# A hybrid decoder layer on one core: the state-space layer's token-independent matrices made beside the first gate/up products and stored, its recurrence stepped at half products

## The chip, the cores and the metric

The kernel runs on one core of a Trainium2 chip. The metric is the time of one execution on the device, in microseconds (us), as the median of several runs. The engines are TensorE (PE; its weight loads are listed apart as PEld), VectorE (DVE), ScalarE (ACT), GpSimd (POOL) and SyncE (SP), which in this kernel issues the data DMAs. Each engine takes its instructions strictly in the order of the program.

## The reference, cut to what matters

One layer over x (1024 tokens x 1024 channels, float32): FFN, mixer of two gated branches, FFN, final norm. The change touches the state-space (S5) branch of the mixer, and the place of the attention branch's work beside it.

```
x = x + 0.5 * swiglu(rms_norm(x, ffn1_norm), ffn1_w_gate, ffn1_w_up, ffn1_w_down)
h = rms_norm(x, mix_norm);  z = h @ w_in
q, k, v, u, g_attn, g_ssm = ...            # slices of z; the gates after a sigmoid
...
# S5: 32 groups of 16 channels, each drives a 64-dim complex diagonal state
bb = coef * b                              # from lam, dt, b: no token enters
s[t] = ab * s[t-1] + bb u[t]               # complex, per group
y_s = gelu(Re(c s) + d u)
glu = y_s @ ssm_w_glu;  y_s = glu[:, :512] * sigmoid(glu[:, 512:])
y_ssm = y_s @ w_ssm_branch
...
# attention: 3 dilated groups of 4 heads; the 3 outputs of a head are mixed by a
# softmax over the groups' log-denominators (lse)
w_grp = softmax(lse over groups);  o_attn = sum(w_grp * o);  y_attn = o_attn @ w_attn_branch
x = x + (g_attn * y_attn + g_ssm * y_ssm) @ w_out
x = x + 0.5 * swiglu(rms_norm(x, ffn2_norm), ...)
```

## The kernel before

**Products.** Every large product is made of three passes over operands that are split into a high and a low part (`mm3`, L179 to L181; `split`, L83 to L90: ACT makes the high part at L86, DVE the low part at L87). Large matrices go by a seven-product scheme on half blocks (`sevens`, L430, sums at L446, L448 and, of weights, at L353). One product of it (`product`, L400) is 12 matmuls on 128x512 tiles; after 6 of them the generator yields `MID`, after 12 it yields again. I call these two places half products.

**Stages.** PE runs through them in this order: the first FFN's gate/up products (`gate_up`, to about 475 us), its down products (`down`, to about 700 us), the mixer's input projection (`project`, to about 1206 us), the state-space branch's output products (`ssm_out`, to about 1334 us), the attention branch's (`attn_out`), the output matrix (`out_product`), and the second FFN.

**Side work.** `run(main, *side, often=())` (L1667) steps through a main generator, and at each of its yields takes one step of each side generator: at `MID` only of those in `often`. So what a side generator issues between two of its yields stands in each engine's queue between two products (or half products) of the main work. Nothing else sets the order.

```
for x in main:
    for s in list(side):
        if (x != MID or s in often) and next(s, "end") == "end":
```

**S5.** Beside the first gate/up products, from step 50 on, `s5_base` (L791) makes the tables that need no token: powers of the diagonal (PW), the input and output matrices (BB, CT). Beside `project`, `s5_all` (L1153) goes through four tiles of eight groups each (`s5_tile`, L1007), one step per product:

1. U, the tile's inputs, are loaded back from DRAM in a regrouped form (L1021, 8 DMAs).
2. Twelve DVE operations on 128x512 (L1034 to L1039) make W (inputs to chunk states) and CA (states to outputs), three to a step. PE transposes W (L1046), ACT copies it into WT.
3. PE makes the taps within a chunk (L1056, L1060); they go through `ks` to DRAM (Kd, L1067) and come back regrouped as KT (L1084, 8 DMAs).
4. PE multiplies U with WT to the chunk's inputs Vs (L1075).
5. The recurrence within a chunk: seven times four DVE operations on 128x128 (L1096 to L1099), two of these sets of four to a step. Then a doubling scan over the chunks' ends (L1108 to L1111) and its spread into the states (L1124, L1125).
6. PE makes the outputs Y from U, KT, Vs and CA (L1136, L1138); they are stored to Yd (L422, 8 DMAs), and the next tile begins.

SP issues all these DMAs in the program's order, the weight loads of the main work (L345 in the projection) among them.

**Attention.** `att_all` (L1373) starts when all four S5 tiles are done. It is in `often`, at a pace that `fast` sets. The two `combine` (L1309), one for each half of the head pairs, mix the groups: loads of lse sums (L1327), a chain of small DVE operations (L1330 to L1342), stores to Ad (L1349), then for each of three groups a load of the output (`uo`, L1357) and two of the weights (`al`, L1359), a POOL multiplication (L1364) and, from the second group on, a POOL addition (L1367); a last split into ohi and olo (L89, L90) feeds `attn_out`. The second `combine` runs beside the last products of `ssm_out`. Between its DMAs the gate loads `gs` (L1492) and the weight loads of the output matrix (L1545) stand on SP.

Of the kernel before, what the change touches and what calls it, by code (L numbers as in the profile page):

```python
# [55 lines left out]
def tile_layer(ctx: ExitStack, tc: tile.TileContext, w, out: bass.AP, taps=None):  # L56
# [676 lines left out]
    def later(n, gen):  # L733
        for _ in range(n):
            yield
        yield from gen
# [264 lines left out]


    Ud, Yd = dt_((4, 128, 1024), "Ud"), dt_((4, 128, 1024), "Yd")

    late5 = Stores()

    def s5_tile(ut):  # L1007
        q4 = slice(4 * ut, 4 * ut + 4)

        def v4(t):  # L1010
            return t.rearrange("p (q j c) -> p q j c", q=4, j=T5)

        def bj(x):
            return x[:, q4, None, :].to_broadcast([128, 4, T5, 16])

        while len(saved) < 5 or ("u", ut) not in saved:
            yield
        yield
        U = slot("U").rearrange("p (g x) -> p g x", g=8)
# [6 lines left out]
        CAv = [CA[:, 512 * i:512 * i + 512] for i in range(2)]  # L1026
        t1 = half_slot("t1")

        def pw(i, lo):
            return PW[:, i, q4, lo:lo + T5, None].to_broadcast([128, 4, T5, 16])  # L1030

        for o, X_, lo, sg in ((W, BB, 0, 1), (CAv, CT, 1, -1)):

            V.tensor_tensor(out=v4(o[0]), in0=bj(X_[:, 0]), in1=pw(0, lo), op=OP.mult)  # L1034
            V.tensor_tensor(out=v4(t1), in0=bj(X_[:, 1]), in1=pw(1, lo), op=OP.mult)
            V.tensor_tensor(out=o[0], in0=o[0], in1=t1, op=OP.subtract if sg > 0 else OP.add)
            V.tensor_tensor(out=v4(o[1]), in0=bj(X_[:, 1]), in1=pw(0, lo), op=OP.mult)
            V.tensor_tensor(out=v4(t1), in0=bj(X_[:, 0]), in1=pw(1, lo), op=OP.mult)
            V.tensor_tensor(out=o[1], in0=o[1], in1=t1, op=OP.add if sg > 0 else OP.subtract)  # L1039
            yield  # L1040

        WT = slot("WT")
        for i in range(2):
            pt = bank(6 + i)
            for q in range(4):
                P.transpose(pt[:, 128 * q:128 * q + 128], W[i][:, 128 * q:128 * q + 128], ident)  # L1046
            A.copy(out=WT[:, 512 * i:512 * i + 512], in_=pt)
        del W, t1, o, X_
        yield

        pk = bank(6)
        for q in range(4):
            o = pk[32 * q:32 * q + 32]
            for i in range(2):
                lh = BD[:, i, 4 * ut + q].rearrange("p a c -> p (a c)")
                P.matmul(o[:, 0:16], lhsT=lh, rhs=CT[:, i, 4 * ut + q, :], start=i == 0, stop=i == 1,  # L1056
                         tile_position=(0, 32 * q))
            for i in range(2):
                lh = BD[:, i, 4 * ut + q].rearrange("p a c -> p (a c)")
                P.matmul(o[:, 16:128], lhsT=lh, rhs=CAv[i][:, 128 * q:128 * q + 112], start=i == 0,  # L1060
                         stop=i == 1, tile_position=(0, 32 * q))
        ks = half_slot("ks")[:, :256]
        G.memset(ks[:, :128], 0.0)
        V.scalar_tensor_tensor(ks[:, 128:144], DEL, DC[:, ut:ut + 1], pk[:, 0:16], op0=OP.mult, op1=OP.add)
        V.tensor_copy(out=ks[:, 144:256], in_=pk[:, 16:128])
        yield
        nc.sync.dma_start(out=Kd[ut], in_=ks)  # L1067
        del ks

        Vs = slot("Vs").rearrange("p (i q m) -> p i q m", i=2, q=4)  # L1070
        for i in range(2):
            pt = bank(6 + i)
            for q in range(4):
                for g2 in range(2):
                    P.matmul(pt[64 * g2:64 * g2 + 64, 128 * q:128 * q + 128],  # L1075
                             lhsT=WT[:, 512 * i + 128 * q + 64 * g2:512 * i + 128 * q + 64 * g2 + 64],
                             rhs=U[:, 2 * q + g2, :], start=True, stop=True)
            A.copy(out=Vs[:, i], in_=pt)
        del WT
        yield  # L1080
        yield
        KT = slot("KT").rearrange("p (g x) -> p g x", g=8)
        for jr in range(T5):
            nc.sync.dma_start(out=KT[16 * jr:16 * jr + 16],  # L1084
                              in_=bass.AP(tensor=Kd.tensor, offset=Kd.offset + ut * 32768 + 16 + 16 * jr,
                                          ap=[[256, 16], [4096, 8], [1, 128]]))

        Vr = Vs.rearrange("p i q (k m) -> p i q k m", m=T5)
        m12 = half_slot("m12")
# [3 lines left out]
        for m in range(1, T5):  # L1093
            cur = Vr[:, :, :, :, m]
            prev = Vr[:, :, :, :, m - 1]
            V.tensor_tensor(out=m1, in0=prev, in1=ar[:, None, :, None].to_broadcast([128, 2, 4, 16]), op=OP.mult)  # L1096
            V.tensor_tensor(out=m2, in0=prev[:, ::-1], in1=AIS[:, :, q4, None].to_broadcast([128, 2, 4, 16]), op=OP.mult)
            V.tensor_tensor(out=m1, in0=m1, in1=m2, op=OP.add)
            V.tensor_tensor(out=cur, in0=cur, in1=m1, op=OP.add)  # L1099
            if m % 2 == 0:  # L1100
                yield

        E = m12[:, 256:384].rearrange("p (i q k) -> p i q k", i=2, q=4)
        V.tensor_copy(out=E[:, :, :, 0:15], in_=Vr[:, :, :, 0:15, T5 - 1])
        for j in range(4):
            n = 15 - (1 << j)
            pr, n1, n2 = E[:, :, :, 0:n], m1[:, :, :, 0:n], m2[:, :, :, 0:n]
            V.tensor_tensor(out=n1, in0=pr, in1=ARE[:, None, q4, j:j + 1].to_broadcast([128, 2, 4, n]), op=OP.mult)  # L1108
            V.tensor_tensor(out=n2, in0=pr[:, ::-1], in1=AIE[:, :, q4, j:j + 1].to_broadcast([128, 2, 4, n]), op=OP.mult)
            V.tensor_tensor(out=n1, in0=n1, in1=n2, op=OP.add)  # L1110
            V.tensor_tensor(out=E[:, :, :, 15 - n:15], in0=E[:, :, :, 15 - n:15], in1=n1, op=OP.add)  # L1111
            if j % 2:
                yield
        t2 = half_slot("t2")[:, :480].rearrange("p (q k m) -> p q k m", q=4, k=15)

        def bE(i):
            return E[:, i, :, 0:15, None].to_broadcast([128, 4, 15, T5])

        def bA(i):
            return AW[:, i, q4, None, :].to_broadcast([128, 4, 15, T5])  # L1120

        for o, a, b, op in ((0, 0, 0, OP.add), (0, 1, 1, OP.subtract), (1, 0, 1, OP.add), (1, 1, 0, OP.add)):
            for q in range(4):
                V.tensor_tensor(out=t2[:, q], in0=bA(a)[:, q], in1=bE(b)[:, q], op=OP.mult)  # L1124
            V.tensor_tensor(out=Vr[:, o, :, 1:16, :], in0=Vr[:, o, :, 1:16, :], in1=t2, op=op)  # L1125
            yield
        del t2, m12, m1, m2, E, n1, n2, pr
# [181 lines left out]
    def combine(hp):  # L1309

        def vw(t, d):
            return t if d == 1 else t.rearrange("p (r i) -> p i r", r=d)

        def nat(t, d):
            return t if d == 1 else t.rearrange("p (i r) -> p i r", r=d)
# [16 lines left out]
        for g, d in enumerate(DIL):  # L1332
            V.tensor_tensor(out=nat(Eg[:, g], d), in0=vw(R[g][:, 0], d), in1=nat(M, d), op=OP.subtract)
        A.activation(out=Eg, in_=Eg, func=AF.Exp)
        for g, d in enumerate(DIL):
# [3 lines left out]
        V.tensor_tensor(out=nat(M, 16), in0=nat(M, 16), in1=vw(R[2][:, 1], 16), op=OP.add)  # L1339
        V.reciprocal(out=M, in_=M)  # L1340
        for g, d in enumerate(DIL):
            V.tensor_tensor(out=vw(AL[:, g], d), in0=nat(Eg[:, g], d), in1=nat(M, d), op=OP.mult)  # L1342
# [431 lines left out]
    def late_half():  # L1774
# [20 lines left out]
    def ssm_first(k):  # L1795
        while len(freed) < k + 1:
# [73 lines left out]
```

## Time and profile before

| what | value |
|---|---|
| median of 3 runs | 2127.29 us (2123.85 to 2128.09) |
| the profiled execution's own time | 2128.07 us |
| span of the profiled execution | 2126.3 us |
| PE busy | 2020.7 us, 95% of the span |
| DVE busy | 1532.4 us, 72% |
| ACT busy | 804.8 us, 38% |
| POOL busy | 432.8 us, 20% |
| DMA moved | 272.07 MB, mean 128 GB/s |

How to read it: PE is the engine that nearly always works, so time is gained only where PE stands still or runs at a lower granted clock, and lost where the change makes it do so. The other engines' totals count only through the places at which PE waits for them. Matmuls overlap, so a busy PE can hide a small loss; the spacing of matmuls shows it, about 0.226 us for one of 128x512 (332 matmuls in a stretch of 75 us without an idle moment).

### The profile page before, as it was taken

Reading aid. Unit: us, or ns where it says so; the run is one execution under the profiler, and the core shown is the slowest. Engines: PE = TensorE matmul, PEld = TensorE weight load, DVE = VectorE, ACT = ScalarE, POOL = GpSimd, SP = SyncE. Lnnn points to the kernel's source line nnn. Section 1 sums busy time; section 2 is a strip of 40 time slices with the busy share of each in tenths; the row PEclk is TensorE's granted clock in tenths of the full one; section 3 lists DMA queues with packets and bytes.
Section 4 is the critical chain, followed back from the end, with each engine's and each line's share of the span. In section 5 each row is a group of like instructions: output and inputs, shape, how many; then the busy total and the mean of one; then the engine's idle time right before and its main releaser. Section 6 shows DMA issues by size and latency. Waiting matters only on the chain. (4 is left out here: it accounts for less than half of the span.)

```text
span 2126.3 us, 26610 instructions
## 1 busy us (share of the span) xinstructions
PE 2020.7 (95%) x9359; PEld 1619.7 (76%) x9359; DVE 1532.4 (72%) x2764; ACT 804.8 (38%) x1534; POOL 432.8 (20%) x380
## 2 busy tenths in 40 slices
PE   6799999999999899999999999998999999999988
PEld 5687888887877687777777667776788888887866
DVE  7778889768867878777855544626876776769776
ACT  5432322325336422222244653435423223235353
POOL 2022112125531000000000324520121121217350
PEclk9899999999999899999999999998999999999999
DMA  4144333329325133333343655431233333266432
GB/s 158 45 129 138 111 99 111 112 96 350 126 76 175 70 119 112 93 111 105 107 146 123 205 165 170 189 109 60 99 99 100 99 124 99 89 217 238 144 116 83
DMA packets 179562, 272.07 MB, mean 128 GB/s; under 512 B 23576, under 2 KB 110436, under 8 KB 179428
## 3 DMA queue, kind: packets, MB, share of 16 engines
q1 hardware_dynamic: 169008, 264.54, 36.7%
q10 hardware_dynamic: 10308, 5.81, 1.1%
q8 instruction: 74, 1.21, 0.2%
q14 instruction: 60, 0.49, 0.1%
q0 software_dynamic: 112, 0.02, 0.1%
HBM read 191.50 MB, written 81.17 MB: 128 GB/s over the span
## 5 line engine op out<-in xcount | busy, mean ns | idle before, releaser
L179 PE MATMUL bank<-T,wp 128*128 128x512 f32 x1008 | 399.8, 397 | 12.5 <-DVE F L309 8.5
L181 PE MATMUL bank<-T,wp 128*128 128x512 f32 x1008 | 396.1, 393 | 9.7 <-DVE wp L87 9.7
L180 PE MATMUL bank<-T,wp 128*128 128x512 f32 x1008 | 395.2, 392 | 0.0
L87 DVE TENSOR_TENSOR wp<-wraw,wp 128x512 fp32r<-128x512 f32 x400 | 329.7, 827 | 71.2 <-ACT wp L86 69.9
L86 ACT CAST wp<-wraw 128x512 fp32r<-128x512 f32 x400 | 244.4, 620 | 279.9 <-DVE wraw L353 161.7
L179 PE MATMUL bank<-b,wp 128*128 128x512 f32 x756 | 303.7, 402 | 17.3 <-DVE s L446 15.5
L181 PE MATMUL bank<-b,wp 128*128 128x512 f32 x756 | 298.4, 395 | 4.7 <-DVE wp L87 4.7
L181 PE MATMUL bank<-wp,ap 128*128 128x512 f32 x744 | 294.0, 395 | 6.8 <-DVE ap L87 6.1
L180 PE MATMUL bank<-b,wp 128*128 128x512 f32 x756 | 297.6, 394 | 0.0
L180 PE MATMUL bank<-wp,ap 128*128 128x512 f32 x744 | 292.4, 393 | 5.3 <-DVE wp L87 5.3
L179 PE MATMUL bank<-wp,ap 128*128 128x512 f32 x744 | 293.0, 394 | 3.6 <-ACT ap L86 2.5
L179 PEld LDWEIGHTS bank<-T,wp 128*128 128x128 f32 x1008 | 190.6, 189 | 57.4 <-issue 15.1
L181 PEld LDWEIGHTS bank<-T,wp 128*128 128x128 f32 x1008 | 190.8, 189 | 53.4 <-DVE wp L87 12.9
L180 PEld LDWEIGHTS bank<-T,wp 128*128 128x128 f32 x1008 | 190.7, 189 | 38.5
L86 ACT CAST wp<-S 128x512 fp32r<-128x512 f32 x189 | 116.7, 618 | 234.7 <-DVE S L353 185.9
L87 DVE TENSOR_TENSOR wp<-S,wp 128x512 fp32r<-128x512 f32 x189 | 150.5, 797 | 71.2 <-ACT wp L86 70.6
L561 POOL TENSOR_TENSOR S<-sg 128x512 f32<-128x512 f32 x22 | 33.7, 1533 | 779.6 <-DVE sg L547 495.5
L179 PEld LDWEIGHTS bank<-b,wp 128*128 128x128 f32 x756 | 144.0, 191 | 54.5 <-ACT wp L86 12.2
L181 PEld LDWEIGHTS bank<-wp,ap 128*128 128x128 f32 x744 | 140.7, 189 | 43.7 <-DVE ap L87 14.9
L181 PEld LDWEIGHTS bank<-b,wp 128*128 128x128 f32 x756 | 143.7, 190 | 38.4 <-DVE wp L87 7.4
L180 PEld LDWEIGHTS bank<-wp,ap 128*128 128x128 f32 x744 | 140.9, 189 | 37.0 <-DVE wp L87 8.1
L179 PEld LDWEIGHTS bank<-wp,ap 128*128 128x128 f32 x744 | 140.8, 189 | 34.3 <-ACT ap L86 3.9
(251 smaller groups left out, 2826.4 us busy)
## 6 DMA issues: line engine op xcount, KB each, us to landing
araw<-aD SPq DMA_DIRECT2D x154, 256.0 KB
wraw<-in_ffn_w_gate_dram SPq DMA_DIRECT2D x44, 512.0 KB
wraw<-in_ffn_w_up_dram SPq DMA_DIRECT2D x44, 512.0 KB
aD<-sg SPq DMA_DIRECT2D x88, 256.0 KB
wraw<-in_ffn_w_down_dram SPq DMA_DIRECT2D x44, 512.0 KB
wraw<-in_w_in_dram SPq DMA_DIRECT2D x38, 512.0 KB
aD<-S SPq DMA_DIRECT2D x66, 256.0 KB
x<-in_x_dram SPq DMA_DIRECT2D x16, 512.0 KB
```

The costliest lines, as they stand in the source:

```text
L86: A.copy(out=hi, in_=src)
L87: (e or V).tensor_tensor(out=lo, in0=src, in1=hi.bitcast(F32), op=OP.subtract)
L179: P.matmul(pt, lhsT=lhs[0], rhs=rhs[0], start=start, stop=False, skip_group_check=more)
L180: P.matmul(pt, lhsT=lhs[0], rhs=rhs[1], start=False, stop=False, skip_group_check=more)
L181: P.matmul(pt, lhsT=lhs[1], rhs=rhs[0], start=False, stop=stop, skip_group_check=more)
L561: G.tensor_tensor(out=ab[o], in0=ab[a], in1=ab[b], op=op)
```

## The change

The twelve DVE operations per tile, the transposes and the taps are taken out of `s5_tile` into a new generator `s5_weights`, which runs right behind `s5_base` as one side generator (`s5_all_weights`) of the first gate/up products, with one DVE operation to a step. WT and CA go to two new DRAM tiles (WTd, CAd) and are loaded by `s5_tile`: WT behind U, CA behind the recurrence together with KT. What is left of this generator when the gate/up products end is stepped beside the first `down`. `s5_all` is now in `often`, so its steps come at half products; the recurrence yields after the two multiplications and again after the two additions. `combine` gets two more yields.

```diff
+    WTd, CAd = dt_((4, 128, 1024), "WTd"), dt_((4, 128, 1024), "CAd")
...
+    def s5_weights():
+        for ut in range(4):
...
+            CAv = []
+            for X_, lo, sg in ((BB, 0, 1), (CT, 1, -1)):
+                for i in range(2):
+                    o, t1 = half_slot("W"), half_slot("t1")
+                    V.tensor_tensor(out=v4(o), in0=bj(X_[:, i]), in1=pw(0, lo), op=OP.mult)
+                    yield
+                    V.tensor_tensor(out=v4(t1), in0=bj(X_[:, 1 - i]), in1=pw(1, lo), op=OP.mult)
+                    yield
+                    V.tensor_tensor(out=o, in0=o, in1=t1, op=OP.subtract if (sg > 0) == (i == 0) else OP.add)
+                    yield
+                    if sg > 0:
+                        pt = bank(6)
+                        for q in range(4):
+                            P.transpose(pt[:, 128 * q:128 * q + 128], o[:, 128 * q:128 * q + 128], ident)
+                        wt = half_slot("WT")
+                        A.copy(out=wt, in_=pt)
+                        late5.add(WTd[ut][:, HALF[i]], wt)
+                    else:
+                        CAv.append(o)
+                        late5.add(CAd[ut][:, HALF[i]], o)
...
+            late5.add(Kd[ut], ks)
+            yield
+    def s5_all_weights():
+        yield from s5_base()
+        for _ in s5_weights():
+            late5.step()
+            yield
...
     def s5_tile(ut):
...
-        W, CA = two("W"), slot("CA")
...
-            yield
-        yield
-        nc.sync.dma_start(out=Kd[ut], in_=ks)
-        del ks
+        nc.sync.dma_start(out=WT, in_=WTd[ut])
+        for _ in range(5):
+            yield
...
             A.copy(out=Vs[:, i], in_=pt)
+            yield
...
             V.tensor_tensor(out=m2, in0=prev[:, ::-1], in1=AIS[:, :, q4, None].to_broadcast([128, 2, 4, 16]), op=OP.mult)
+            yield
             V.tensor_tensor(out=m1, in0=m1, in1=m2, op=OP.add)
             V.tensor_tensor(out=cur, in0=cur, in1=m1, op=OP.add)
-            if m % 2 == 0:
-                yield
+            yield
+        KT, CA = slot("KT").rearrange("p (g x) -> p g x", g=8), slot("CA")
...
+        nc.sync.dma_start(out=CA, in_=CAd[ut])
...
         A.activation(out=Eg, in_=Eg, func=AF.Exp)
+        yield
...
         V.tensor_tensor(out=nat(M, 16), in0=nat(M, 16), in1=vw(R[2][:, 1], 16), op=OP.add)
+        yield
         V.reciprocal(out=M, in_=M)
...
-    drain(run(gate_up(H, late_half()), later(30, other_gains()), later(40, bias_tables()), later(50, s5_base())))
+    side = run(gate_up(H, late_half()), later(30, other_gains()), later(40, bias_tables()), later(50, s5_all_weights()))
...
-    drain(run(down(NF // 2, tile_of(xin), 0.5, *normed(X1), half0),
+    drain(run(down(NF // 2, tile_of(xin), 0.5, *normed(X1), half0), *side,
...
-    side = run(project(H, later(0, h_seven(1, 1, (1, 2, 6, 7), H)), freed), s5_all(),
+    side = run(project(H, later(0, h_seven(1, 1, (1, 2, 6, 7), H)), freed), s5,
...
-               often=(att,))
+               often=(att, s5))
```

Three places show how this moves instructions. The first is DVE's queue at the start of the first `down`, where the last tile's operations stand between the low halves of the main work (L87, `wp` of one factor and `ap` of the other). Before, nothing else stood there:

```order
L87 TENSOR_TENSOR wp<-wraw,wp 128x512
L87 TENSOR_TENSOR ap<-araw,ap 128x512
L87 TENSOR_TENSOR wp<-wraw,wp 128x512
L87 TENSOR_TENSOR ap<-araw,ap 128x512
L87 TENSOR_TENSOR wp<-wraw,wp 128x512
L87 TENSOR_TENSOR ap<-araw,ap 128x512
```

With the change, rows 741 to 751 of that queue are:

```order
L87 TENSOR_TENSOR wp<-wraw,wp 128x512
L87 TENSOR_TENSOR ap<-araw,ap 128x512
L1032 TENSOR_TENSOR W<-W,t_4219 128x512
L87 TENSOR_TENSOR wp<-wraw,wp 128x512
L87 TENSOR_TENSOR ap<-araw,ap 128x512
L1028 TENSOR_TENSOR W<-CT,PW 128x512
L1030 TENSOR_TENSOR t_4294<-CT,PW 128x512
L1032 TENSOR_TENSOR W<-W,t_4294 128x512
L1028 TENSOR_TENSOR W<-CT,PW 128x512
L87 TENSOR_TENSOR wp<-wraw,wp 128x512
L87 TENSOR_TENSOR ap<-araw,ap 128x512
```

Of the 48 moved operations 17 stand behind the end of the gate/up products; PE's queue has that end at position 1848, and the last matmul of the main work ahead of the last of the 17 operations' users at position 2017.

The second place is SP's queue in the projection, between the stores of one tile's Y and the first loads of the next. Before:

```order
L422 DMA Pdq<-pr 128x1024 x2
L422 DMA Yd<-Y 16x8x128 x8
L1021 DMA U<-Ud 16x8x128 x8
L345 DMA wraw<-in_w_in_dram 128x4x256 x2
L422 DMA Pdk<-pr 128x1024
L1067 DMA Kd<-ks 128x256
L422 DMA Pdk<-pr 128x1024
L1084 DMA KT<-Kd 16x8x128 x8
```

With the change:

```order
L422 DMA Pdq<-pr 128x1024 x2
L422 DMA Yd<-Y 16x8x128 x8
L1080 DMA U<-Ud 16x8x128 x8
L1083 DMA WT<-WTd 128x1024
L345 DMA wraw<-in_w_in_dram 128x4x256 x2
L422 DMA Pdk<-pr 128x1024 x2
L345 DMA wraw<-in_w_in_dram 128x4x256 x2
L422 DMA Pdv<-pr 128x1024 x2
```

WT (512 KB) is loaded right behind U; in the next tile one weight load stands between the stores of Y and U as well. On PE, the first matmuls of Vs (L1075, now L1092) stood 72 matmuls of the main work behind the previous tile's last Y matmul, and now stand 42 behind it (tiles 1 to 3).

The third place is the second `combine` on SP. Before, four gate loads (`gs`) stand behind the first load of `uo`:

```order
L1349 DMA Ad<-c_10671 8x16x8 x2
L1492 DMA gs<-Gd 128x1024
L1357 DMA uo<-Od 128x1024
L1359 DMA al<-Ad 64x1024 x2
L1545 DMA wraw<-in_w_out_dram 128x1024
L1492 DMA gs<-Gd 128x1024 x2
L1357 DMA uo<-Od 128x1024
L1359 DMA al<-Ad 64x1024 x2
L1545 DMA wraw<-in_w_out_dram 128x1024
L1492 DMA gs<-Gd 128x1024 x2
L1357 DMA uo<-Od 128x1024
L1359 DMA al<-Ad 64x1024 x2
```

With the change one does, and three loads of the first `combine` (`uo`, `al` x2) now stand ahead of the second one's lse loads:

```order
L1371 DMA Ad<-c_10798 8x16x8 x2
L1567 DMA wraw<-in_w_out_dram 128x1024
L1514 DMA gs<-Gd 128x1024
L1379 DMA uo<-Od 128x1024
L1381 DMA al<-Ad 64x1024 x2
L1514 DMA gs<-Gd 128x1024
L1567 DMA wraw<-in_w_out_dram 128x1024
L1379 DMA uo<-Od 128x1024
L1381 DMA al<-Ad 64x1024 x2
L1379 DMA uo<-Od 128x1024
L1381 DMA al<-Ad 64x1024 x2
```

The attention's last matmul (L1240, now L1260) moves as well: it stood in front of the last 210 main matmuls of `ssm_out`, and now stands in front of the last 168. The number of main matmuls is the same, 8004.

## Rows read from the trace of the kernel before

**Rows 1.** Profile page, part 1: busy time, share, instructions of each engine.

```profile
PE 2020.7 (95%) x9359; PEld 1619.7 (76%) x9359; DVE 1532.4 (72%) x2764; ACT 804.8 (38%) x1534; POOL 432.8 (20%) x380
```

**Rows 2.** Stretches: length, busy time (count) of each engine, PE clock, DMA share, GB/s.

```profile
200.00:400.00 200.00, 198.21 (x877) 162.97 (x876) 171.34 (x387) 56.79 (x101) 32.42 (x22) 1.00 0.35 108
400.00:475.00 75.00, 75.00 (x332) 62.10 (x332) 50.96 (x69) 24.61 (x44) 12.09 (x8) 1.00 0.34 113
475.00:500.00 25.00, 25.00 (x111) 20.42 (x110) 17.09 (x21) 9.25 (x15) 6.47 (x5) 1.00 0.90 343
500.00:510.00 10.00, 10.00 (x45) 8.26 (x45) 7.98 (x7) 7.78 (x15) 7.96 (x6) 1.00 1.03 414
510.00:560.00 50.00, 48.48 (x210) 38.72 (x209) 50.00 (x42) 22.12 (x38) 37.18 (x23) 1.00 0.44 156
786.00:1090.00 304.00, 286.48 (x1483) 225.90 (x1483) 233.78 (x513) 80.02 (x136) 0.62 (x3) 0.99 0.36 114
```

**Rows 3.** PE's waits, 786 to 1090 us: total us, times, longest us.

```profile
PE bank L181 <- DVE wp L87: 8.0, 8, 2.2
PE bank L179 <- DVE s L446: 4.8, 4, 2.6
PE bank L179 <- DVE pr L1432: 3.9, 2, 2.4
```

**Rows 4.** Timeline of DVE inside the recurrence: start us, us, operation.

```profile
809.13 0.39 DVE L1096 TENSOR_TENSOR m<-Vs,AW 128x128 f32<-128x128 f32 x1
...
810.64 0.40 DVE L1096 TENSOR_TENSOR m<-Vs,AW 128x128 f32<-128x128 f32 x1
...
812.03 0.68 DVE L87 TENSOR_TENSOR wp<-S,wp 128x512 fp32r<-128x512 f32 x1
...
813.37 0.39 DVE L1096 TENSOR_TENSOR m<-Vs,AW 128x128 f32<-128x128 f32 x1
...
817.46 0.39 DVE L1096 TENSOR_TENSOR m<-Vs,AW 128x128 f32<-128x128 f32 x1
```

**Rows 5.** Stretches at 733, 737 and 976 us, columns as in rows 2.

```profile
733.50:737.50 4.00, 0.57 (x3) 0.15 (x1) 4.00 (x7) 1.53 (x3) 0.00 (x0) 1.00 0.00 0
737.50:744.30 6.80, 5.38 (x13) 4.21 (x14) 6.73 (x12) 3.23 (x7) 0.00 (x0) 0.50 0.00 0
976.40:979.80 3.40, 3.40 (x10) 2.63 (x9) 3.30 (x8) 0.00 (x0) 0.00 (x0) 0.50 0.31 107
```

**Rows 6.** Groups of PE's weight loads, 780 to 1090 us: busy, mean ns, idle before.

```profile
L1056 PEld LDWEIGHTS bank<-CT,BD 128*32 128x32 f32 x64 | 2.7, 110 | 1.4 <-issue 1.4
```

**Rows 7.** Timeline of DVE at the start of `down`.

```profile
500.27 0.68 DVE L87 TENSOR_TENSOR ap<-araw,ap 128x512 fp32r<-128x512 f32 x1
500.93 1.72 DVE L87 TENSOR_TENSOR wp<-wraw,wp 128x512 fp32r<-128x512 f32 x1
502.58 1.77 DVE L87 TENSOR_TENSOR ap<-araw,ap 128x512 fp32r<-128x512 f32 x1
```

**Rows 8.** Timeline of PE where tile 0's Y ends.

```profile
856.22 0.50 PE L179 MATMUL bank<-T,wp 128*128 128x512 f32 x1
```

**Rows 9.** Timeline of SP's queue there: start us, us of issuing.

```profile
860.70 3.70 SPq L1021 DMA_DIRECT2D U<-Ud  x8
864.73 0.40 SPq L345 DMA_DIRECT2D wraw<-in_w_in_dram  x1
```

**Rows 10.** The stretch behind that load, columns as in rows 2.

```profile
868.20:870.80 2.60, 2.60 (x13) 2.01 (x12) 2.57 (x5) 1.34 (x3) 0.00 (x0) 1.00 0.00 0
```

**Rows 11.** Timelines at the end of `ssm_out`: PE, SP, POOL and ACT.

```profile
1335.75 0.49 PE L179 MATMUL bank<-ohi,whi 128*128 128x512 f32 x1 [0.72 <-ACT ohi L89]
...
1306.11 1.09 SPq L1359 DMA_DIRECT2D al<-Ad  x2
...
1313.57 2.40 POOL L1364 TENSOR_TENSOR o<-uo,al 128x1024 f32<-128x1024 f32 x1 [10.71 <-DMA al<-Ad]
...
1321.33 2.40 POOL L1364 TENSOR_TENSOR al<-uo,al 128x1024 f32<-128x1024 f32 x1 [3.00 <-DMA al<-Ad]
1323.81 2.97 POOL L1367 TENSOR_TENSOR o<-o,al 128x1024 f32<-128x1024 f32 x1
...
1334.64 1.06 ACT L89 ACTIVATE ohi<-o 128x1024 fp32r<-128x1024 f32 x1 [8.77 <-POOL o L1367]
```

More of the change, by code (lines that the diff above doesn't have):

```diff
@@ L1003, in tile_layer, with v4, bj, pw @@
     Ud, Yd = dt_((4, 128, 1024), "Ud"), dt_((4, 128, 1024), "Yd")
+    WTd, CAd = dt_((4, 128, 1024), "WTd"), dt_((4, 128, 1024), "CAd")
     late5 = Stores()
+    def v4(t):
+        return t.rearrange("p (q j c) -> p q j c", q=4, j=T5)
+    def s5_weights():
+        for ut in range(4):
+            q4 = slice(4 * ut, 4 * ut + 4)
+            def bj(x):
+                return x[:, q4, None, :].to_broadcast([128, 4, T5, 16])
+            def pw(i, lo):
+                return PW[:, i, q4, lo:lo + T5, None].to_broadcast([128, 4, T5, 16])
+            CAv = []
[18 more added lines that the diff above has]
+                        late5.add(CAd[ut][:, HALF[i]], o)
+            pk = bank(6)
+            for q in range(4):
+                o = pk[32 * q:32 * q + 32]
+                for i in range(2):
+                    lh = BD[:, i, 4 * ut + q].rearrange("p a c -> p (a c)")
+                    P.matmul(o[:, 0:16], lhsT=lh, rhs=CT[:, i, 4 * ut + q, :], start=i == 0, stop=i == 1,
+                             tile_position=(0, 32 * q))
+                for i in range(2):
+                    lh = BD[:, i, 4 * ut + q].rearrange("p a c -> p (a c)")
+                    P.matmul(o[:, 16:128], lhsT=lh, rhs=CAv[i][:, 128 * q:128 * q + 112], start=i == 0,
+                             stop=i == 1, tile_position=(0, 32 * q))
+            ks = half_slot("ks")[:, :256]
+            G.memset(ks[:, :128], 0.0)
+            V.scalar_tensor_tensor(ks[:, 128:144], DEL, DC[:, ut:ut + 1], pk[:, 0:16], op0=OP.mult, op1=OP.add)
+            V.tensor_copy(out=ks[:, 144:256], in_=pk[:, 16:128])
+            late5.add(Kd[ut], ks)
+            yield
@@ L1007, in s5_tile @@
+    def s5_all_weights():
[3 more added lines that the diff above has]
+            yield
+        for _ in range(3):
+            late5.step()
+            yield
     def s5_tile(ut):
         q4 = slice(4 * ut, 4 * ut + 4)
[L1010 to L1014, printed above, removed]
         while len(saved) < 5 or ("u", ut) not in saved:
@@ L1018, in s5_tile @@
         yield
-        U = slot("U").rearrange("p (g x) -> p g x", g=8)
+        U, WT = slot("U").rearrange("p (g x) -> p g x", g=8), slot("WT")
         for jr in range(T5):
@@ L1023, in s5_tile @@
                                           ap=[[1024, 16], [16384, 8], [1, 128]]))
-        W, CA = two("W"), slot("CA")
[L1026 to L1039, printed above, removed]
-            yield
[L1042 to L1048, printed above, removed]
-        yield
[L1051 to L1065, printed above, removed]
-        yield
-        nc.sync.dma_start(out=Kd[ut], in_=ks)
-        del ks
+        nc.sync.dma_start(out=WT, in_=WTd[ut])
+        for _ in range(5):
+            yield
         Vs = slot("Vs").rearrange("p (i q m) -> p i q m", i=2, q=4)
@@ L1078, in s5_tile @@
             A.copy(out=Vs[:, i], in_=pt)
+            yield
         del WT
         yield
-        yield
[L1082 to L1086, printed above, removed]
         Vr = Vs.rearrange("p i q (k m) -> p i q k m", m=T5)
@@ L1097, in s5_tile @@
             V.tensor_tensor(out=m2, in0=prev[:, ::-1], in1=AIS[:, :, q4, None].to_broadcast([128, 2, 4, 16]), op=OP.mult)
+            yield
             V.tensor_tensor(out=m1, in0=m1, in1=m2, op=OP.add)
             V.tensor_tensor(out=cur, in0=cur, in1=m1, op=OP.add)
-            if m % 2 == 0:
-                yield
+            yield
+        KT, CA = slot("KT").rearrange("p (g x) -> p g x", g=8), slot("CA")
+        CAv = [CA[:, 512 * i:512 * i + 512] for i in range(2)]
+        for jr in range(T5):
+            nc.sync.dma_start(out=KT[16 * jr:16 * jr + 16],
+                              in_=bass.AP(tensor=Kd.tensor, offset=Kd.offset + ut * 32768 + 16 + 16 * jr,
+                                          ap=[[256, 16], [4096, 8], [1, 128]]))
+        nc.sync.dma_start(out=CA, in_=CAd[ut])
         E = m12[:, 256:384].rearrange("p (i q k) -> p i q k", i=2, q=4)
@@ L1124, in s5_tile @@
                 V.tensor_tensor(out=t2[:, q], in0=bA(a)[:, q], in1=bE(b)[:, q], op=OP.mult)
+            yield
             V.tensor_tensor(out=Vr[:, o, :, 1:16, :], in0=Vr[:, o, :, 1:16, :], in1=t2, op=op)
@@ L1334, in combine @@
         A.activation(out=Eg, in_=Eg, func=AF.Exp)
+        yield
         for g, d in enumerate(DIL):
@@ L1339, in combine @@
         V.tensor_tensor(out=nat(M, 16), in0=nat(M, 16), in1=vw(R[2][:, 1], 16), op=OP.add)
+        yield
         V.reciprocal(out=M, in_=M)
```

3 lines of the change are left out of this document (1 added, 2 removed).

## The prediction

> **What bounds the kernel now.** I read the busy times first. PE works 95% of the span [rows 1], so a change can give at most what PE loses at single places, and the next view has to be by stage. The table of stretches [rows 2] shows that PE has no idle moment from 400 to 475 us, the end of the first gate/up products (75.00 busy of 75.00), but only 286.48 us of 304.00 in the four S5 tiles: 17.5 us idle, with DVE busy 233.78. The list of waits [rows 3] names the causes there: low halves (L87) 8.0 us, sums (L446) 4.8, projections' outputs (L1432) 3.9, together 16.7 of the 17.5. All are small DVE operations of the main work that come late. They are late because S5's own operations are queued in front: the timeline of DVE [rows 4] shows two recurrence sets from 809.13 to 812.03, at a spacing of 1.51 us (809.13 to 810.64), then 1.34 us of main work to 813.37. One product of the projection is 12 matmuls at 0.226 us (75.00 us for 332 [rows 2]), 2.71 us, and while the recurrence lasts DVE needs 4.2 us for each (809.13 to 817.46 is 8.33 us for two). So in these tiles DVE is the bound, by bursts, and outside them PE is.
>
> **The change part by part.** The sum is made against the profiled execution's 2128.07 us; the median of the three runs, 2127.29, is 0.8 lower. A measurement of this kernel can tell about 0.2%, 4.3 us, from no change.
>
> *The projection, gain.* The 48 operations on 128x512 leave, and the recurrence is spread from two sets per product to one. DVE's need falls from 4.2 us per product to 1.51 + 1.34 = 2.85, against PE's 2.71. Nearly in step, with 0.14 us too much in each of seven products per tile: 1 us a tile that the buffered operands mostly absorb. I leave 1.5 us of the 17.5 standing. A fall of the granted clock goes too: the stretch at 976.40 us has PEclk 0.50 for 3.40 us [rows 5], which is 1.7 us lost, in the tile with waits up to 2.6 us. That makes -17.7; ends -19.2 (all of it goes) and -9 (only the waits for sums and outputs go, 4.8 + 3.9 = 8.7, and the low halves' 8.0 stay).
>
> *Change-overs on PE.* The transposes and taps cost PE the same in their new place. But each change from one kind of matmul to another costs an issue gap: 1.4 us at four places before the taps [rows 6], 0.35 each. Before, a tile had five such blocks; now four remain and three stand in the gate/up products, eight more in all: +2.8 (0 if they hide behind running matmuls, 4 if some cost half more).
>
> *The gate/up products.* Of the moved operations 31 fall into their end. At 0.61 us spacing (812.03 to 813.37 holds two and a pause [rows 4]) that is 18.9 us into 24.0 us that DVE has free there (75.00 less 50.96 [rows 2]): covered on average. The stretch before, 200 to 400 us, ran `s5_base` with DVE 171.34 of 200 and lost PE 1.8 us [rows 2]; over 75 us at a similar load I take +1 (0 to 3).
>
> *The first `down`.* The other 17 fall here, 10.4 us. DVE has free 25.00 - 17.09 = 7.9 us until 500, then 10.00 - 7.98 = 2.0 until 510, and nothing behind: 50.00 of 50.00 [rows 2]. So the cover is just used up, and whoever is late then is L87, for which PE waits. Beyond that DVE is slower here: L87 takes 0.68 us, and 1.72 or 1.77 when its neighbours show POOL at work [rows 7], which is busy 6.47 of 25 us and then 7.96 of 10 [rows 2]. Eleven of the 17 in the first stretch at a share of 0.26 and six in the second at 0.8 make eight slow ones, 8 x 1.09 = 8.7 us more. Stores of WT and CA, six halves of 256 KB here, meet DMA queues that are full (share 1.03 at 414 GB/s, so 3.8 us for 1.57 MB [rows 2]). Ends 0 (buffered low halves cover it) and 13 (10.4 - 9.9 + 8.7 + 3.8, all paid); I take +4, since POOL is mostly idle while two thirds of them run.
>
> The Trainium skill, page "GPSIMD Engine Reference", section "1. Specifications", says that GpSimd shares its SBUF interfaces with VectorE and contends with DVE instructions that have two SBUF inputs; every moved operation has two. By that rule all eight under POOL are slow, and with nothing absorbed this term would be 9.2 us instead of 4. The trace agrees that the same L87 has two durations [rows 7]; that S5's operations have them too, no row here shows.
>
> *The new wait of Vs.* Before, W was made while U was on its way, and Vs came late enough. Now Vs waits for WT, which is issued right behind U. After the previous tile's last Y, PE has 42 matmuls of main work: 856.22 + 9.5 = 865.7 us [rows 8]. SP issues U from 860.70 for 3.70 us, so WT can go at 864.4 [rows 9]. The weight load issued at 864.73, of the same 512 KB, has landed by 868.2, where DMA shows 0.00 [rows 10]: 3.4 us. WT is there at 867.8, 2.1 us late. Behind Vs on PE stands the main work, so PE waits. Tiles 1 to 3 pay, tile 2 with one more load in front (0.40 to issue): 6.7, rounded to +7. Ends 0 (SP is earlier) and 12 (each tile waits for the whole 3.4 us and loses some clock). A wait this short costs no clock: waits of 2.2 us stand beside a PEclk of 0.99 [rows 2, 3].
>
> *The second `combine`.* S5's steps are spread out, so attention's last matmul has 42 main matmuls fewer behind it: 9.5 us less cover for the chain lse loads, softmax, Ad, three outputs, ohi, olo, on which `attn_out` waits. Before, the chain ended 0.72 us too late already [rows 11], so there is no slack. Three loads of the first `combine` now go ahead of the lse loads; such loads take SP 0.4 to 0.5 us each (1.09 for two [rows 11]): +1.5. Three of four gate loads that stood between the outputs' loads are past, so POOL's wait of 3.00 us for `al` may go: -3.0. Together +8.0; ends 3 (from 1313.57 to 1334.64 us POOL has 21.1, of which its own three multiplications and two additions, 2.40 x 3 + 2.97 x 2, are 13.1 [rows 11], so 8.0 us can go) and 13 (nothing shortens, and the two added yields each hold the chain back by some of a product). Then the clock: after PE stood nearly all of 4.0 us, 6.8 us ran at 0.50 [rows 5], 3.4 lost. A wait of 8 us gets this too: +11.4 in all (3 to 16.4).
>
> Sum: -17.7 + 2.8 + 1 + 4 + 7 + 11.4 = +8.5, so 2136.6, and 0.8 less for the median: **2136 us**.
>
> **The rivals.**
>
> *The queue on SP runs ahead (other side: faster).* Where W's steps are gone, SP has less to wait for, and U, WT and the last `al` are issued earlier. It decides at 2.1 us: if WT goes at 862.3 instead of 864.4, no tile waits, and if the same holds at the end, the chain shortens by the whole 8.0 us, leaving 3, too little for a fall of the clock. -17.7 + 2.8 + 1 + 4 + 0 + 3 = -6.9: 2120.4. For it: the queue's order has fewer gate loads between `uo` and `al`. Against: U follows the stores of Y in both kernels, and those wait for the same ACT work.
>
> *One of the two new waits is covered.* If the chain of `combine` is covered, 2124.4; if only WT is in time, 2128.8. Both within 0.2%.
>
> *The change doesn't do what it says.* DVE in finer steps is still late, 2.85 us against 2.71, and the eight L87 waits stay [rows 3]: the gain is 9 instead of 17.7, 2144.5.
>
> *DVE and POOL collide in `down`* in full: 9.2 us instead of 4, 2141.
>
> **How the numbers follow.** My own sum 0.33; SP ahead 0.21; one wait covered 0.26; steps still late 0.12; the collision 0.08. Faster is the SP case, 0.21; the same 0.26; slower 0.33 + 0.12 + 0.08 = 0.53. The range goes from 2117 (the SP case with all 19.2 gained and a little over) to 2147 (the late steps and some of the upper ends). Of the two largest unknown prices, the chain's spans 13 us and WT's 12, so it can't be narrower.
>
> **What would show it.** In the projection, PE's waits for L446 and pr gone and L87's near 1 us; three waits on the first Vs matmul of about 2 us each, released by the DMA of WT; one wait of 7 to 9 us for ohi ahead of `attn_out`, with PEclk 0.50 behind it; PE waits of a few us for L87 around 480 to 515 us. I am wrong if PE passes from Vs without a wait, if ohi is ready within 1 us of the last product of `ssm_out`, or if waits of more than 8 us remain in the projection.

## The result, and the profile after

The changed kernel takes 2137.53 us (median of 4 runs, 2133.55 to 2139.41), the kernel before 2125.58 beside it: ratio 1.0053, 95% interval 1.0032 to 1.0073. It is slower by half a per cent; the forecast was 2136. The profiled execution of the change took 2138.97 us, with a span of 2137.0.

PE's total has hardly moved (part 1 of the page, against [rows 1]), so the loss again lies in single places:

```profile
PE 2019.3 (94%) x9359; PEld 1625.8 (76%) x9359; DVE 1531.9 (72%) x2764; ACT 802.8 (38%) x1534; POOL 433.3 (20%) x380
```

The 8004 matmuls of the main work are the same in every kernel of this study, and in the same order. So the start of the n-th of them, minus its start in the kernel before (in us), tells how far a kernel is behind (+) or ahead at that place, worked out from the traces by counting:

| main matmul | place | after | weights only | steps only | no added yields | seven before Vs |
|---|---|---|---|---|---|---|
| 1847 | end of gate/up | +5.8 | +5.0 | +0.5 | +6.7 | +5.1 |
| 2770 | end of `down` | +12.3 | +11.7 | +0.4 | +12.5 | +13.2 |
| 4360 | end of the projection | -17.2 | +2.0 | -14.1 | -16.2 | -18.7 |
| 4750 | end of `ssm_out` | -3.8 | +2.1 | -0.9 | -3.1 | -14.3 |
| 4775 | in `attn_out` | +12.8 | +1.7 | +9.3 | +8.3 | -10.5 |
| 8003 | last | +10.7 | -1.2 | +6.8 | +7.3 | -11.5 |

(The columns on the right are experiments, below.) The change loses 12.3 us ahead of the mixer, of which much is moved PE work. It gains 29.5 in the projection, part of it attention work that now lies behind it in `ssm_out` (13.4 us come back there), and loses 16.6 at one place, the start of `attn_out`.

PE's waits in the four S5 tiles (786 to 1090 us; total us, times, longest us) answer to [rows 3]. All three causes named there are gone, and one line has taken their place:

```profile
PE bank L1092 <- DMA WT<-WTd: 9.7, 3, 4.1
```

The timeline of PE shows each of the three; in brackets the idle time before and what ended it:

```profile
877.16 1.52 PE L1092 MATMUL bank<-U,WT 128*64 128x128 f32 x16 [2.46 <-DMA WT<-WTd]
...
952.35 1.61 PE L1092 MATMUL bank<-U,WT 128*64 128x128 f32 x16 [4.07 <-DMA WT<-WTd]
...
1026.63 1.09 PE L1092 MATMUL bank<-U,WT 128*64 128x128 f32 x16 [3.15 <-DMA WT<-WTd]
```

The stretches (columns as in [rows 2]) show the whole of it, and what the granted clock did behind each wait:

```profile
786.00:1090.00 304.00, 294.32 (x1404) 238.81 (x1403) 207.25 (x467) 78.18 (x132) 0.00 (x0) 0.98 0.41 130
874.50:877.40 2.90, 0.44 (x5) 0.27 (x6) 0.63 (x2) 0.00 (x0) 0.00 (x0) 1.00 0.93 310
877.90:880.90 3.00, 3.00 (x13) 2.20 (x10) 0.00 (x0) 0.58 (x1) 0.00 (x0) 0.50 0.94 329
953.00:956.30 3.30, 3.30 (x16) 2.39 (x12) 1.16 (x2) 1.10 (x2) 0.00 (x0) 0.52 0.94 366
1028.00:1031.30 3.30, 3.30 (x16) 2.28 (x16) 0.00 (x0) 0.93 (x2) 0.00 (x0) 0.50 0.53 205
```

PE idles 9.7 us instead of 17.5, but each of these waits of 2.5 to 4.1 us is followed by over 3 us at half clock (0.50, which is 1.2 instead of 2.4 GHz). That is about 1.7 us more, three times.

At the end of `ssm_out` the rows of PE, POOL, DVE and ACT answer to [rows 11]:

```profile
1346.54 0.80 PE L179 MATMUL bank<-ohi,whi 128*128 128x512 f32 x1 [15.29 <-ACT ohi L89]
...
1327.14 2.40 POOL L1386 TENSOR_TENSOR o<-uo,al 128x1024 f32<-128x1024 f32 x1 [13.52 <-DMA al<-Ad]
...
1334.90 2.34 POOL L1386 TENSOR_TENSOR al<-uo,al 128x1024 f32<-128x1024 f32 x1 [3.01 <-DMA al<-Ad]
...
1303.24 2.98 POOL L1389 TENSOR_TENSOR o<-o,al 128x1024 f32<-128x1024 f32 x1
...
1301.35 2.07 DVE L1350 TENSOR_TENSOR c<-c 16x128 f32<-16x128 f32 x1
1303.45 3.03 DVE L1351 TENSOR_TENSOR c<-c 16x128 f32<-16x128 f32 x1
...
1345.43 1.06 ACT L89 ACTIVATE ohi<-o 128x1024 fp32r<-128x1024 f32 x1 [16.45 <-POOL o L1389]
```

PE waits 15.29 us for the second `combine`, where it waited 0.72, and behind that wait the clock is low again:

```profile
1346.50:1352.50 6.00, 5.50 (x13) 4.02 (x14) 3.21 (x4) 6.00 (x8) 1.40 (x2) 0.53 0.81 332
```

POOL's wait of 3 us between the outputs has not gone. And DVE's addition at 1303.45, on 16x128, takes 3.03 us while POOL finishes the first `combine` at 1303.24.

### The profile page after: what moved, and what is told of

The parts are those of the page before. It is cut to its first block, busy times and chain, and to the rows that moved or that the text cites. A ratio compares the mean times of both kernels' runs of the same rounds, so it can differ in the third digit from the quotient of the medians.

```text
span 2137.0 us, 26602 instructions
## 1 busy us (share of the span) xinstructions
PE 2019.3 (94%) x9359; PEld 1625.8 (76%) x9359; DVE 1531.9 (72%) x2764; ACT 802.8 (38%) x1534; POOL 433.3 (20%) x380
## 5 line engine op out<-in xcount | busy, mean ns | idle before, releaser
L87 DVE TENSOR_TENSOR wp<-wraw,wp 128x512 fp32r<-128x512 f32 x400 | 327.5, 822 | 71.5 <-ACT wp L86 70.1
L87 DVE TENSOR_TENSOR wp<-S,wp 128x512 fp32r<-128x512 f32 x189 | 150.8, 798 | 72.1 <-ACT wp L86 71.7
L181 PEld LDWEIGHTS bank<-wp,ap 128*128 128x128 f32 x744 | 140.7, 189 | 41.7 <-DVE ap L87 12.9
```

Of the source, the lines that this page charges most:

```text
L87: (e or V).tensor_tensor(out=lo, in0=src, in1=hi.bitcast(F32), op=OP.subtract)
L181: P.matmul(pt, lhsT=lhs[1], rhs=rhs[0], start=False, stop=stop, skip_group_check=more)
```

## The experiments

**One part at a time.** *Weights only*: the matrices are moved and stored, S5's steps and `combine` are those of before.

```diff
-               often=(att, s5))
+               often=(att,))
...
-            yield
...
-            yield
+            if m % 2 == 0:
+                yield
```

> The matrices are moved and stored as in the change, but the state-space tiles step at whole products as before, with two recurrence sets to a step, and combine has no added yields; attention's last matmul stands again where it stood before the change. My theory (the waits in the projection come from the recurrence, two sets per product, and not from the moved operations): PE's waits for low halves, sums and outputs between the tiles stay, 14 to 17 us of 17.4; no wait for WT (four products behind the load); ohi late by at most 2 us; the first gate/up and down lose the same 12 us as in the change. Time: 2125.6 + 12.4, less 8 for PE work taken out of the projection, less 0 to 3: 2127 to 2130. Rival (the moved operations had used up DVE's lead, so the recurrence ran late): waits under 8 us, time 2116 to 2120.

Measured: 2128.66 us, ratio 1.001 (0.9997 to 1.0023): no difference. PE's waits in the tiles are those of [rows 3] almost to the digit:

```profile
PE bank L181 <- DVE wp L87: 7.5, 6, 2.2
PE bank L179 <- DVE s L446: 4.5, 3, 2.6
PE bank L179 <- DVE pr L1451: 3.9, 2, 2.4
```

So the recurrence, two sets to a product, made these waits, and not the twelve operations that were moved. The table shows the price of the move: 11.7 us up to the end of `down`, of which 9.7 come back in the projection, 2 net. The moved work alone gains nothing.

*Steps only*: the kernel before with the finer steps and `often`, the matrices still made in the tiles.

```diff
+            yield
             V.tensor_tensor(out=m1, in0=m1, in1=m2, op=OP.add)
             V.tensor_tensor(out=cur, in0=cur, in1=m1, op=OP.add)
-            if m % 2 == 0:
-                yield
+            yield
...
-               often=(att,))
+               often=(att, s5))
```

> The kernel before with the finer steps alone: the state-space tiles step at half products, the matrices are still made in the tiles, combine has no added yields. Attention's last matmul stands 42 main matmuls later, as in the change. My theory (the attention branch's wait comes from the steps, and the waits in the projection go with the steps): waits in the projection 17.4 -> under 5 us; no wait for WT, since there is none to load; ohi late by 10 to 15 us, with a half clock behind it; first gate/up and down unchanged against before. Time: 2125.6 - 13 - 2 + 13 + 1 = 2122 to 2128. Rival (three moved operations in one half product are as bad as two recurrence sets in a product): new waits of 5 us or more where W and CA are made, time 2128 to 2133. Second rival (the late ohi belongs to the moved matrices' loads): ohi late by under 3 us, time about 2112.

Measured: 2137.16 us, ratio 1.0053 (1.0037 to 1.0069). My time missed, and so did the rivals'; the first rival was right about the tiles, and my own theory about the end. PE's waits in the tiles, and below them the one at `attn_out`:

```profile
PE bank L1060 <- DVE CA L1039: 6.2, 4, 1.6
PE bank L1046 <- DVE W L1039: 4.2, 4, 1.3
PE bank L1060 <- DVE CA L1036: 2.5, 4, 1.5
...
PE bank L179 <- ACT ohi L89: 9.5, 1, 9.5
```

The recurrence's waits are gone, but with three operations to a half product W and CA come 12.9 us late. So the parts need each other here: the move makes the finer steps usable, and only the steps gain. (A kernel that makes W and CA in the tiles with one operation to a step was not run.) The late ohi, 9.5 us, comes with the steps alone; no WT is loaded in this kernel.

**The late ohi.** *No added yields* in `combine`:

```diff
         A.activation(out=Eg, in_=Eg, func=AF.Exp)
-        yield
...
-        yield
         V.reciprocal(out=M, in_=M)
```

> The change without the two yields added to combine. The chain from the store of the last attention output to ohi took 52.4 us in the change and 48.0 before, though fewer loads stand in it. My theory: the yields let three operations of the main work in front of the reciprocal (1.20 + 2 x 0.67 us), so the wait for ohi falls from 15.3 to 12 to 14 us and the time by 2 to 3, to 2135. Rival (each yield holds the chain by most of a product): 15.3 -> 9 to 11 us, time 2131 to 2133. Rival (the chain's small DVE operations are slow because POOL works beside them, 2.07 and 3.03 us instead of 1.23 and 0.39, and the yields do nothing): 15.3 within 0.7, time unchanged.

Measured: 2132.26 us, ratio 1.0026 (1.0014 to 1.0037). ohi is late by 9.7 us instead of 15.3, so the yields cost 5.6. The size is that of the first rival, but its reason isn't all of it. The yields also put off the first `combine`, so that its last loads go ahead of the second one's and its last POOL operations run beside the second one's small DVE operations. Without them POOL stands still there, and DVE's timeline reads:

```profile
1303.21 0.38 DVE L1350 TENSOR_TENSOR c<-c 16x128 f32<-16x128 f32 x1
1303.62 0.40 DVE L1351 TENSOR_TENSOR c<-c 16x128 f32<-16x128 f32 x1
```

0.38 and 0.40 us, against 2.07 and 3.03 in the change. The Trainium skill, page "GPSIMD Engine Reference", section "1. Specifications", names this contention for DVE instructions with two SBUF inputs. This pair of traces agrees with it. The rest, 9.7 us, is the cover that the later attention lost, as in the run with the steps alone (9.5).

**The price ahead of the mixer.** *Weights earlier*: `later(50, ...)` becomes `later(30, ...)`.

> The change with the generator of the tables and matrices started at step 30 of the first gate/up products instead of 50, so that all 48 operations, their transposes and taps lie inside the gate/up products (main matmuls 1236 to 1812 of 1848) and none in down. My theory: down loses nothing any more against before (6.6 us in the change, of which some 2.8 is PE work that now lies in gate/up, and 3.8 is lateness: 2.9 a PE wait for W); gate/up takes 8 to 9 us of moved PE work instead of 5.8. Time 3 to 5 us less than the change: 2133 to 2135. Rival (gate/up pays it in the same way, since DVE has no more room there): time unchanged, with new PE waits for L87 or W of 3 us or more before 480 us.

Measured: 2145.25 us, ratio 1.0086 (1.007 to 1.0102), about 8 us worse than the change: wrong in size and in sign. `down` indeed loses nothing any more (21.5 us behind at matmul 1847, 21.0 at 2770), but 7.9 us are lost by matmul 1000, long before the first moved operation. PE's waits from 160 to 200 us show where:

```profile
PE bank L179 <- DVE z L50: 5.6, 1, 5.6
```

L50 belongs to the tables' small operations, which now fall together with those of the bias tables, and the clock is at 0.50 from 187.0 to 190.4 us. And what `down` gets back, the gate/up products pay, as the rival had it: from matmul 1000 to 2770 this kernel loses 13.1 us and the change 12.2, and PE's wait for W, 2.9 us in `down`, is one of 2.6 in gate/up. Whether another start would do better was not run.

**The wait for WT.** *U and WT ahead*: both are loaded for the next tile behind KT and CA (`ahead` issues the eight loads of U and the one of WT).

```diff
         nc.sync.dma_start(out=CA, in_=CAd[ut])
+        if ut < 3:
+            ahead(ut + 1)
```

> The change with U and WT of the next tile loaded one tile ahead (behind KT and CA of the tile before), nothing else moved: the steps and the place of attention are those of the change. My theory (PE waits on the landing of WT, and each of the three waits brings 3.4 us at half clock): the waits of 9.7 us and the three spells, 3 x 1.7 us, go; ohi stays late by 14 to 16 us, since the cover behind attention is counted in products. Time 2137.5 - 13 to 15: 2122 to 2125. Rival (SP's queue only hands the lateness on: nine more loads ahead of the stores and weight loads of the tile): new PE waits on KT, CA or wp of 5 us or more, time 2130 or more.

Measured: 2156.22 us, ratio 1.0128 (1.0102 to 1.0154), the rival and worse. No wait for WT is left in the tiles, but a larger one has come:

```profile
PE bank L179 <- ACT wp L86: 17.6, 6, 6.4
```

These are the casts of the main work's weights. Where PE waited longest for one (6.29 and 6.39 us), ACT itself stood still until a store of the projection's outputs had landed:

```profile
867.98 0.62 ACT L86 CAST wp<-S 128x512 fp32r<-128x512 f32 x1 [8.97 <-DMA Pdq<-pr]
...
948.75 0.62 ACT L86 CAST wp<-S 128x512 fp32r<-128x512 f32 x1 [9.06 <-DMA Pdq<-pr]
```

Two runs on top of it, *ahead, short* (no five half products before Vs) and *ahead, short, plain* (no added yields in `combine` either), aimed at the end:

> As the run with U and WT loaded ahead, and the five steps of waiting before Vs are left out for tiles 1 to 3, so that attention's last matmul stands at 4530 main matmuls (4542 before the change, 4584 in the change). Combine keeps its two added yields. My theory (cover counted in products, yields worth 5.6 us): the wait for ohi falls from 15.3 us to 3 to 6 us. Time 2122 to 2125, less 9 to 12: 2111 to 2115. Rival (DVE's small operations of the chain, slow beside POOL, are the larger part): ohi stays late by 8 us or more, time 2117 or more.

> As the run before it, and combine's two added yields are taken out too: the moved matrices and the finer steps stay, the two new waits should be gone. My theory: ohi late by at most 2 us, no wait for WT, no waits for low halves, sums and outputs between the tiles; what stays of the change against the kernel before is +2 us from the moved work and -19 from the steps. Time 2107 to 2111, faster than both kernels. Rival (the gain of the steps is partly given back elsewhere once the two waits are gone, to DMA or ACT): 2114 or more.

Measured: 2162.07 and 2159.78 us (1.0154, 1.0128 to 1.018; 1.0152, 1.0128 to 1.0176). The times are spoilt by the late casts, 25 us of such waits in both. At `attn_out` the theory of the cover holds: ohi late by 4.5 us with the yields, and not at all without them.

I held that two buffers kept longer starved the weight loads. *WT alone ahead* and then *U's buffer taken early, its loads where they were* were to tell:

> The change with WT alone loaded a tile ahead, so that one buffer of 512 KB is held longer instead of two, and one DMA instead of nine is moved on SP. My theory (with U and WT ahead the weight loads waited for buffers, 50.3 us of waits for L87 against 30.4, and PE for the cast of late weights): one held buffer costs about half of it, PE waits for L86 of 5 to 12 us, U on its own lands in time within 1 us, ohi late by 14 to 16 us; time 2137.5 - 15 + 5 to 12, which is 2128 to 2135. Rival (it was the eight loads of U put ahead in SP's queue that held the weight loads): no wait for L86, time 2121 to 2125.

> As the run with WT alone loaded ahead, and the next tile's buffer for U is taken at the same point too, but its eight loads stay where they were in SP's queue. It tells apart why loading U ahead cost so much. My theory (a second buffer held through the tile starves the weight loads): PE waits for the high half L86 (1.4 us with WT alone ahead, 17.6 with U's loads ahead) come back, 10 us or more, time 2140 or more. Rival (the eight loads themselves, ahead of the weight loads in SP's queue): L86 within 1 us of 1.4, time within 4 us of 2131.3.

Measured: 2131.3 us (1.0018, 1.0008 to 1.0027) and 2130.09 (1.001, 0.9999 to 1.0021). The waits of both are the same; those of the second:

```profile
PE bank L1099 <- DMA U<-Ud: 3.4, 3, 1.8
PE bank L179 <- ACT wp L86: 1.4, 2, 0.7
```

So held buffers cost next to nothing, and my theory fell: it is U's eight loads, put ahead of other DMAs on SP, that cost 16 us. The trace tells part of how: these casts wait for stores, not for weight loads. A store of Pdv, ahead of a cast for which PE waits 2.75 us, is issued behind U's loads at 839.84 us, and at 835.28 where the loads stay. The store of Pdq ahead of the first cast above follows at 862.87 instead of 850.59, behind weight loads that waited for L87. That the casts need the buffers that these stores free is argued, not shown. WT one tile ahead, on the other hand, takes the 9.7 us and the half clock away, for 3.4 us of waits on U; ohi stays late by 15.3 and 14.2.

*WT before U*, and *seven* or *six* half products before Vs. All three go without the added yields and give the doubling scan one half product per round, so that attention ends early enough again.

```diff
-        for _ in range(5):
+        for _ in range(7 if ut else 5):
...
             V.tensor_tensor(out=n2, in0=pr[:, ::-1], ...
-            yield
             V.tensor_tensor(out=n1, in0=n1, in1=n2, op=OP.add)
```

> The change with three edits of its steps and none of its loads: in tiles 1 to 3 seven instead of five half products stand between the loads and Vs (12 matmuls, 2.7 us, more cover for WT); the doubling scan takes one half product per round instead of two, so that attention's last matmul stands at 4548 main matmuls (4542 before the change, 4584 in it); combine has no added yields. No buffer is held longer, unlike in the runs with loads ahead. My theory: waits for WT of 9.7 us fall to 0 to 3 us with at most one spell at half clock, ohi is late by at most 3 us, the scan costs 0 to 3 us of new waits for L87. Time 2108 to 2114, faster than both kernels. Rival (any loading of WT behind U starves the weight loads, as loads ahead did): waits for the high half L86 of 8 us or more, time 2120 or more.

> As the run before it in the scan and in combine, but five half products before Vs as in the change, and WT is issued ahead of the eight loads of U instead of behind them: WT lands 3.7 us earlier, U's last load 0.4 us later. Attention's last matmul stands at 4524. My theory (512 KB of WT are what Vs waits for, not the queue as such): the wait on WT goes and one on U takes its place, 0 to 1.5 us each, without half clock; time 2107 to 2113. Rival (U's small packets share the DMA engines with WT and land late): waits on U of 2 us or more each, with half clock, 2115 to 2122.

> As the run with seven half products before Vs, but with six: 6 matmuls, 1.4 us, less cover for WT per tile, and attention's last matmul 18 main matmuls earlier. My theory: two or three waits for WT of 1 to 2.5 us, with one or two spells at half clock (1.7 us each); ohi late by less than 1 us instead of 2.9; time within 4 us of 2115.2: 2113 to 2119. Rival (WT's landing comes no sooner than Vs in any case, since SP is held by the stores of Y): no difference in the waits for WT, 2112 to 2114.

*Seven* measured 2115.18 us, ratio 0.9932 (0.992 to 0.9944): faster than both kernels. Its three edits were not run one by one, except for the yields above. PE's waits in the tiles and at `attn_out` come first, then the stretch of the tiles, with columns as in [rows 2]:

```profile
PE bank L179 <- DVE s L448: 1.3, 1, 1.3
PE bank L1092 <- DMA wraw<-in_w_in_dram: 1.0, 1, 1.0
PE bank L179 <- DVE s L446: 0.8, 1, 0.8
PE bank L1092 <- issue: 0.4, 1, 0.4
...
PE bank L179 <- ACT ohi L89: 2.9, 1, 2.9
```

```profile
786.00:1090.00 304.00, 300.48 (x1455) 240.78 (x1454) 216.28 (x498) 86.44 (x155) 0.00 (x0) 1.00 0.45 140
```

3.5 us idle in 304 instead of 17.5, at full clock. The scan with two operations more to a step can have cost at most the 2.1 us of waits for sums (L448, L446).

*WT before U* measured 2131.25 us (1.0009, 0.9999 to 1.0019), the rival in kind, but past its 2115 to 2122: the wait only changed its name, `DMA U<-Ud: 9.9, 3, 4.0`. Whichever of the two is issued last is waited for. More is lost beside attention, which begins earlier still in this kernel: one wait of 6.0 us for DVE, with the clock at 0.50 from 1211.4 to 1221.6 us.

*Six* measured 2124.91 us (0.9991, 0.9979 to 1.0002), outside my 2113 to 2119. Its waits at Vs are 1.9 us for WT and 4.1 that the list calls issue, without half clock, and ohi isn't late at all. 7 us more than with seven are lost beside attention, which begins 18 matmuls earlier here: PE's waits there are 8.4 us (3.1 and 2.9 for DVE, 2.4 for ACT) against 3.3 with seven, and the clock is at 0.50 for 6.8 us (1202.4 to 1209.2) against 3.4. Why attention fares worse at that place wasn't followed.

## Why the prediction was right, by its steps

The forecast was +8.5 us against the profiled execution; the trace's last matmul is +10.7, and the medians beside each other are 12.0 apart. The mechanisms were the right ones, but four sizes were off, by 1 to 8 us each, and made up for each other. That the total came so near is luck.

- *The projection, -17.7.* Right: of 17.4 us of waits none is left, and the fall of the clock at 976 us (1.7 us) is gone, -19.1. That the waits belong to the recurrence is shown by the run with the weights alone, where they stay. "The buffered operands mostly absorb" the 0.14 us too much per product: all of it.
- *Change-overs, gate/up and `down`, +2.8 + 1 + 4 = +7.8.* Too high. The run with the weights alone is 2.1 us behind at matmul 4750, where all moved work has been done. The single terms were not separated. In `down` the waits for L87, my sign, did not grow (4.2 us from 475 to 700 us, 4.8 before). Instead PE waited 2.9 us for W, and some of the moved operations were slow there, as the groups of DVE from 475 to 530 us show (busy us, mean ns, idle before):

```profile
L1032 DVE TENSOR_TENSOR W<-W,t 128x512 f32<-128x512 f32 x6 | 7.4, 1232 | 0.0
L1028 DVE TENSOR_TENSOR W<-CT,PW 128x512 f32<-128x512 f32 x4 | 2.7, 682 | 0.0
```

  But what the projection got back was more than I had counted.
- *The wait of Vs, +7.* The place and the number of waits were right. They are 9.7 us in the list, 2.5 to 4.1 each instead of 2.1. In tile 1 WT was issued at 873.10 us, 1.6 us ahead of its turn on PE (1.3 in the forecast), but Vs began 4.1 us behind the issue, where I had 3.4. And the sentence "A wait this short costs no clock" failed: each brought over 3 us at half clock, 1.7 lost, so about 14.8 in all. The mean of 0.99 in [rows 2] on which it rested already holds such a spell, the one at 976.40 us in [rows 5], which begins 1.0 us behind a wait of 2.42 us.
- *The second `combine`, +11.4.* 16.6 (from -3.8 to +12.8): the wait grew by 14.6 where I had 8.0, and the low clock behind it cost 2.0 where I had 3.4. The lost cover was rightly counted (9.5 us; without the yields the wait is 9.5 and 9.7, which is 8.8 and 9.0 more than before). What failed is the chain itself. I let it shorten by 3.0 because fewer gate loads stand in it, and POOL's wait is still 3.01 us. And I kept the two added yields for the upper end alone; they cost 5.6. The chain before the first multiplication on POOL, from the store of the last attention output, took 26.9 us before, 34.2 in the change and 27.0 without the yields. Behind it POOL took 2.8 us less, since one operation of the main work (`wlo`) stands there instead of two. My lower end of 3 overlooked these two: 4.8 of the 8.0 us that I let go were theirs. Before:

```profile
1286.63 0.34 SPq L1273 DMA_DIRECT2D Od<-Uo  x1
...
1315.93 2.40 POOL L87 TENSOR_TENSOR wlo<-wraw,whi 128x1024 fp32r<-128x1024 f32 x1
...
1326.72 2.41 POOL L87 TENSOR_TENSOR wlo<-wraw,whi 128x1024 fp32r<-128x1024 f32 x1
```

  With the change:

```profile
1292.98 0.34 SPq L1293 DMA_DIRECT2D Od<-Uo  x1
...
1329.51 2.39 POOL L87 TENSOR_TENSOR wlo<-wraw,whi 128x1024 fp32r<-128x1024 f32 x1
```

- The rival on the other side, with SP running ahead, would have needed WT 2.1 us earlier. It came later than forecast. Of the rival that collides DVE with POOL in `down` the run shows some, an estimated 3.8 us at most (the 6.6 us that `down` loses, less 2.8 of moved PE work).

The terms as measured make -19.1 + 2.1 + 14.8 + 16.6 = 14.4 at the start of `attn_out`, where the count of matmuls says 12.8; the 1.6 between them stay open. Another 2.1 us were gained behind that place, which no step of mine names; 1.0 of them comes where the clock is at 0.50 for 10.2 us (1475.0 to 1485.2) instead of 13.7 (1461.1 to 1474.8 before).

## What to carry to other kernels

A finer interleaving of side work gains where the main engine waits for a helper's bursts, but it also stretches the side work, and what stands last in line loses its cover: count that cover in main instructions behind the last side instruction, before and after. A result that is stored and loaded again needs a landing time of its own in the schedule, here 2.7 us more of main work (seven steps instead of five). Reloads put further ahead in an in-order queue can cost more than the wait that they remove.

## What the runs showed of the hardware

For waits of 2 to 3 us, the length of a single wait of PE does not tell whether the granted clock falls behind it. Of one and the same wait, for the sum of L446 in the last tile, the kernel before shows no fall:

```profile
1049.31 0.47 PE L179 MATMUL bank<-b,wp 128*128 128x512 f32 x1 [2.64 <-DVE s L446]
...
1049.30:1052.70 3.40, 3.36 (x14) 2.50 (x15) 3.23 (x14) 0.00 (x0) 0.00 (x0) 1.00 0.11 39
```

In the run with the weights only the wait is as long, and the clock is at 0.50 behind it:

```profile
1050.33 0.77 PE L179 MATMUL bank<-b,wp 128*128 128x512 f32 x1 [2.62 <-DVE s L446]
...
1050.30:1053.60 3.30, 3.27 (x8) 2.62 (x9) 3.13 (x13) 0.00 (x0) 0.00 (x0) 0.50 0.18 65
```

So the half clock behind a short wait is a cost that can come or not; the wait of 2.32 us for WT in the run without the yields had none, the one of 2.46 us in the change had it.

A small DVE operation on 16x128 took 3.03 us while POOL worked, and 0.40 when POOL stood still.
